# Planning the order of all engines through the attention of a two-layer hybrid transformer, with two modulation blocks moved into the merge

## The chip, the cores and the metric

The kernel runs on one core of one Trainium2 chip. The metric is device time in microseconds (us): the median over runs of one launch, from the first instruction to the last. Five engines work side by side: TensorE (PE in the profile: matrix products, with PEld for its weight loads), VectorE (DVE), ScalarE (ACT), GpSimd (POOL) and SyncE (SP), which here only issues DMAs. Each engine takes its instructions in the order in which the program lists them, and waits on semaphores for the others.

## The reference

Two layers over 512 latent tokens and 256 context tokens of width 1024, in float32. Cut to what matters:

```python
for l in range(DEPTH):                                   # DEPTH = 2
    mod = silu_c @ w_mod[l] + b_mod[l]                   # 1024 -> 6*1024, and mod_c from silu_cc for the context
    sh1, sc1, g1, sh2, sc2, g2 = jnp.split(mod[:, None, :], 6, axis=-1)
    h = modulate(rms_norm(x, norm1[l]), sh1, sc1)        # and hc from ctx
    na_q, na_k, na_v, gq, gk, gv, ga, gb = jnp.split(h @ w_in[l], IN_SPLITS, axis=-1)
    ya = neighbourhood attention of 8 heads              # windows of 8x16 on the 64-wide grid, bias, all context keys
    qb = apply_rope(rms_norm(heads(gq), q_gain[l]))      # kb likewise, from gk
    yb = grouped-query attention of 8 heads on 2 key heads
    x = x + g1 * ((sigmoid(ga) * (ya @ w_pa[l]) + sigmoid(gb) * (yb @ w_pb[l])) @ w_o[l])
    # the same for the context tokens, in layer 0 only
    h2 = modulate(rms_norm(x, norm2[l]), sh2, sc2)
    x = x + g2 * swiglu(h2, w_ffn_in[l], w_ffn_out[l])   # and the context, in layer 0 only
return rms_norm(x, final_norm)
```

`mod` is a matrix product with one row: each of its 48 blocks of 128 outputs is a weight block of 512 KB.

## The kernel before

**Products.** Each float32 operand is split into a high and a low part, and a product is three matmuls: high by high, high by low, low by high. For a weight, `weight` loads `wr`, ACT copies it to `wh` (L369), and POOL subtracts to give `wl` (L371; the first key weight of layer 1 goes through `kh` on ACT, L1277, and `kl` on DVE, L1278). `steps` (L384) issues the matmuls, in the order `h,wh`, `hl,wh`, `h,wl` for each of 8 blocks of 128 rows.

**Stages.** Per layer: normalization and first keys, attention, merge of the two branches with `w_pa` and `w_pb` (`pp`, `mb`, L1585), output projection, and the feed-forward part (FFN: `qu`, `qv`, `qc` in, `po` out). In layer 0 the columns are 512 latent and 256 context tokens, in layer 1 the queries are the latent ones only.

**Attention.** A stream of attention items gives scores (`sc`), on DVE the maximum per row (`m`, L1048, times the row factor `hr`, L1054), on ACT the exponential with its sum (`p`, L1056), on DVE the scaling by the reciprocal (`rc`, `p`), on PE the transposes (`tp`), on ACT and DVE their high and low halves (`pth` L1016, `ptl` L1017), and on PE the product with the values (`y`). Between these, the class `Flow` puts the matmuls of the projections that later heads need ("fillers": `pj`, `pv`, `k`, `v`, `q`, and the branch gates). Query and key vectors get a row factor from a sum of squares (`st` on PE, `hr` on DVE, a power on POOL, L807) and a rotation (`rope`: a shuffle `sh` on DVE, its product with `sin_sb`, on POOL or DVE, a product with `cos_sb` and an addition on DVE).

**What sets the order before.** `Flow` models the engines as lines of work and decides, as the program is written, which matmul comes next. Attention stands in a manual schedule for PE alone: PE's order is the written one, and the framework's scheduler places the instructions of the four other engines, as early as its own rules let them come.

**Modulation blocks.** A block of `wmodT` is reduced on DVE against the vector `crow`: two reductions of 128x1024 for each of layer 0's blocks in question (one for the latent, one for the context vector; L452), each followed by a read of the sum. `MODS` says after how many steps of the merge (first branch, second branch) and of the output projection how many blocks are reduced; layer 0 has 24 there, and the rest of the first 48 is reduced in the FFN, before its output needs the gate vector `G` (L478). The DMA of each block is issued by SP in the order of the rows.

Of the kernel before, what the change touches and what calls it, by code (L numbers as in the profile page):

```python
# [20 lines left out]
P = 128  # L21
D = 1024
KB = D // P
S = 512
# [46 lines left out]
MODS = (((0, 1, 1, 1, 1, 1, 0, 1), (1, 1, 2, 2, 2, 2, 1, 0), (1, 1, 1, 1, 1, 1, 1, 0)),  # L71
# [54 lines left out]


# [20 lines left out]
class Flow:  # L148
# [4 lines left out]
    def __init__(self, fillers, live, pace, hop, slow):  # L153
# [9 lines left out]
        self.lines = {e: Line() for e in "avg"}  # L163

# [3 lines left out]
    def go(self, t, *ops):  # L168

        for e, n in ops:  # L170
            fixed, each, on = RATE[e]
            t = self.lines[on].take(t + self.hop, (fixed + n * each) * self.slow["avg".index(on)])
        return t + self.hop
# [29 lines left out]
    def fill(self):  # L203
# [4 lines left out]
        if f.state == 0:  # L208
            next(f.steps)
# [4 lines left out]
        try:  # L214
            v = next(f.steps)
        except StopIteration:
# [8 lines left out]
        else:  # L225
            self.clock += v
# [5 lines left out]
    def ahead(self):  # L232

        for f in self.fillers:
            if f.state == 1:
                return
            if f.state == 0:
                next(f.steps)
                f.state = 1
                return  # L240

# [10 lines left out]
    def run(self, steps):  # L252
        mine = 0.0
        self.ahead()
        for v in steps:
            if isinstance(v, Until):
                self.wait(v.t)
            else:
                self.clock += v
# [8 lines left out]
    def force(self, ready):  # L268
        while not ready():
            if not self.fill():  # L270
                self.rest(self.clock + 0.5)

# [62 lines left out]
class Trunk:  # L335
    def __init__(self, tc, nc, dram):
        self.tc, self.nc, self.d = tc, nc, dram
# [12 lines left out]
    def ps(self, tag, n="ps", cols=512):  # L350
        if tag not in self.pbufs:
            tag = "a" if tag == "g" else "t" if "t" in self.pbufs else "n"
        return self.psum[tag].tile([P, cols], F32, tag=tag, bufs=self.pbufs[tag], name=self.name(n))
# [441 lines left out]
    def roped(self, t):  # L795
        return self.go(("v", S), ("g", S), ("v", S), ("v", S), at=t)
# [24 lines left out]
    def gqa_k(self, l, h, spans, pool, out):  # L821
# [25 lines left out]
        end = self.roped(flow.clock + 0.7)  # L847
        self.rope(kg, pool)
        yield Until(end - self.plan["soon"])
# [44 lines left out]
    def gqa_q(self, l, j, h, spans, pool, out):  # L894
# [14 lines left out]
        end = max(end, self.roped(flow.clock - 1.0))  # L909
        nr = self.small.tile([P, 16], F32, tag="hr", name=self.name("nr"))  # L910
        nc.vector.tensor_scalar(nr[:, : n // HD], r[:, : n // HD], -1.0, None, op0=ALU.mult)
        self.rope(qg, pool)
        yield Until(end - self.plan["soon"])
# [116 lines left out]
    def gqa_pair(self, head, q, kk, val, out, i, pool, done=None):  # L1030
# [20 lines left out]
        def exp(s, b, at):  # L1051
# [4 lines left out]
            nc.scalar.activation(p, s[:, :T], AF.Exp, bias=m[:, 0:1], scale=nr[:, c : c + 1], accum_out=m[:, 1:2])  # L1056
            self.soften(p, m[:, 1:2], pool)
            ps_.append(p)
            end = self.go(("v", 1), ("e", T), at=at)
# [27 lines left out]
    def ctx_item(self, head, score, val, out, r, nr, v, pool, done):  # L1087
# [4 lines left out]
        def soft(s, at):  # L1092
# [7 lines left out]
            for b in range(2):  # L1100
# [4 lines left out]
                self.soften(p[:, c], m[:, 2 + b : 3 + b], pool)  # L1105
            ps_.append(p)
            end = self.go(("v", S), ("v", 1), ("e", 256), ("e", 256), at=at)
            return end, self.go(("v", 1), ("v", 1), ("w", 256), ("w", 256), at=end - 0.5)
# [45 lines left out]
    def na_pair(self, head, q, k, val, bias, out, i, pool, done=None):  # L1154
# [16 lines left out]
        def soft(s, b, at):  # L1171
# [7 lines left out]
                halves(z[:]), halves(s[:, 0:512]), add, 1.0, BIG, ALU.add, ALU.min, m[:, 0:1])  # L1179
# [1178 lines left out]
```

## Time and profile before

| | |
|---|---|
| time, median of 3 runs | 1950.61 us (1950.57 to 1950.74) |
| the profiled execution | 1951.55 us; its span 1949.8 us, so 1.75 us lie around it |
| PE busy | 1913.6 us, 98% of the span |
| DVE, ACT, POOL busy | 1472.3, 943.6, 226.7 us |
| mean granted clock of PE | 0.995 |

Layer 0's attention lies at about 67 to 427 us of the span, its merge at 427 to 544, its FFN at 612 to 1135; layer 1's attention lies at about 1135 to 1458. A row of the timeline has the start and the duration in us, the engine, the line, the operation and its tiles (`out<-in`), and in brackets how long the engine had been idle and which instruction ended that. A row of the windows has the window, its length, then for each engine the busy time and the number of instructions, and behind them the clock that PE was granted (1.00 is full speed), the share of the DMA engines and the rate. A matmul's duration in the rows includes its filling of the array, so that the next starts before it ends: the step from start to start is what it costs.

### The profile page before, as it was taken

Reading aid. Unit: us, or ns where it says so; the run is one execution under the profiler, and the core shown is the slowest. Engines: PE = TensorE matmul, PEld = TensorE weight load, DVE = VectorE, ACT = ScalarE, POOL = GpSimd, SP = SyncE. Lnnn points to the kernel's source line nnn. Section 1 sums busy time; section 2 is a strip of 40 time slices with the busy share of each in tenths; the row PEclk is TensorE's granted clock in tenths of the full one; section 3 lists DMA queues with packets and bytes.
Section 4 is the critical chain, followed back from the end, with each engine's and each line's share of the span. In section 5 each row is a group of like instructions: output and inputs, shape, how many; then the busy total and the mean of one; then the engine's idle time right before and its main releaser. Section 6 shows DMA issues by size and latency. Waiting matters only on the chain.

```text
span 1949.8 us, 31489 instructions
## 1 busy us (share of the span) xinstructions
PE 1913.6 (98%) x12298; PEld 1778.2 (91%) x12298; DVE 1472.3 (76%) x2802; ACT 943.6 (48%) x1822; POOL 226.7 (12%) x131
## 2 busy tenths in 40 slices
PE   8999999999999989999999998999999999999998
PEld 8989999998899989999999888889988999999998
DVE  7468887769778877787868577888657688777785
ACT  5466666642236523342424345666553355444553
POOL 0332222214200000000000012322310000000000
PEclk9999999999999999999999999999999999999999
DMA  8121112234452143334443411121235532332332
GB/s 327 44 70 43 51 59 63 76 114 162 161 212 87 66 130 109 117 122 133 138 141 134 158 65 55 47 60 55 79 103 172 201 109 74 100 115 92 102 98 83
DMA packets 71669, 210.85 MB, mean 108 GB/s; under 512 B 8544, under 2 KB 10720, under 8 KB 71520
## 3 DMA queue, kind: packets, MB, share of 16 engines
q1 hardware_dynamic: 71520, 208.84, 32.6%
q8 instruction: 96, 1.57, 0.3%
q14 instruction: 53, 0.43, 0.1%
HBM read 196.75 MB, written 6.82 MB: 104 GB/s over the span
## 4 chain that ended last, share of the span: by engine, by line
PE 91%; DVE 5%; issue 2%; ACT 1%; DMA 1%; SPq 0%; POOL 0%; DVEq 0%; POOLq 0%; ACTq 0%
PE po L384 21%; PE pj L384 19%; PE qu L1740 14%; PE qv L1740 7%; PE pp L384 6%; PE qc L1740 3%; PE pv L957 3%; PE pf L384 3%; PE y L1076 2%; PE sc L1040 2%; PE tp L1066 2%; PE y L1203 2%; PE sc L1167 2%; PE tp L1191 1%; PE pj L680 1%
## 5 line engine op out<-in xcount | busy, mean ns | idle before, releaser
L1740 PE MATMUL qu<-r,w 128*128 128x384 f32 (+1 forms) x1872 | 295.0, 310 | 0.0
L1740 PEld LDWEIGHTS qu<-r,w 128*128 128x128 f32 x1872 | 281.1, 190 | 3.6 <-DVE tt L2219 2.4
L384 PE MATMUL pj<-h,wh 128*128 128x512 f32 (+1 forms) x704 | 257.4, 366 | 3.3 <-ACT kg L816 1.7
L384 PE MATMUL pj<-h,wl 128*128 128x512 f32 (+1 forms) x704 | 247.6, 352 | 0.0
L384 PE MATMUL pj<-hl,wh 128*128 128x512 f32 (+1 forms) x704 | 247.1, 351 | 0.0
L384 PE MATMUL po<-ph,wh 128*128 128x512 f32 (+1 forms) x576 | 198.4, 344 | 5.9 <-ACT wh L1907 5.9
L369 ACT ACTIVATE wh<-wr 128x1024 fp32r<-128x1024 f32 (+1 forms) x131 | 124.6, 954 | 161.2 <-issue 44.6
L384 PE MATMUL po<-ph,wl 128*128 128x512 f32 (+1 forms) x576 | 197.3, 343 | 0.0
L384 PE MATMUL po<-pl,wh 128*128 128x512 f32 (+1 forms) x576 | 197.0, 342 | 0.0
L1603 ACT ACTIVATE w<-wr 128x512 fp32r<-128x512 f32 x234 | 145.5, 625 | 103.9 <-DVE wr L2183 37.2
L371 POOL TENSOR_TENSOR wl<-wr,wh 128x1024 fp32r<-128x1024 f32 (+1 forms) x67 | 151.1, 2261 | 370.7 <-ACT wh L369 370.6
L1595 DVE SCALAR_TENSOR_TENSOR x<-po,G,x 128x256 f32<-128x256 f32 (+3 forms) x168 | 99.4, 597 | 102.5 <-PE po L384 101.3
L1607 DVE TENSOR_TENSOR w<-wr,w 128x512 fp32r<-128x512 f32 x234 | 159.3, 686 | 10.7 <-ACT w L1603 9.8
L1740 PE MATMUL qv<-r,w 128*128 128x384 f32 (+1 forms) x936 | 150.7, 310 | 0.3 <-ACT tt L1746 0.3
L384 PEld LDWEIGHTS pj<-h,wl 128*128 128x128 f32 x704 | 133.4, 189 | 18.0
L384 PEld LDWEIGHTS pj<-h,wh 128*128 128x128 f32 x704 | 133.7, 190 | 17.5 <-ACT kg L816 1.9
L384 PEld LDWEIGHTS pj<-hl,wh 128*128 128x128 f32 x704 | 133.9, 190 | 13.5
L1740 PEld LDWEIGHTS qv<-r,w 128*128 128x128 f32 x936 | 141.2, 190 | 0.5 <-ACT tt L1746 0.5
L1016 ACT ACTIVATE pth<-tp 128x512 fp32r<-128x512 f32 x176 | 103.2, 595 | 65.7 <-PE tp L1066 37.5
L512 POOL TENSOR_TENSOR rs<-rs,expo 128x2 f32<-128x2 f32 (+2 forms) x8 | 6.2, 773 | 1106.8 <-DVE rs L511 1106.8
L1017 DVE TENSOR_TENSOR ptl<-tp,pth 128x512 fp32r<-128x512 f32 x176 | 119.4, 684 | 18.4 <-ACT pth L1016 16.9
L384 PEld LDWEIGHTS po<-ph,wh 128*128 128x128 f32 x576 | 109.0, 189 | 18.9 <-ACT wh L1907 6.1
(255 smaller groups left out, 4331.5 us busy)
## 6 DMA issues: line engine op xcount, KB each, us to landing
wr<-wfi SPq DMA_DIRECT2D x88, 512.0 KB, 3.3
wr<-wmodT SPq DMA_DIRECT2D x84, 512.0 KB, 3.4
wr<-win SPq DMA_DIRECT2D x68, 512.0 KB, 3.4
wr<-wfo SPq DMA_DIRECT2D x64, 256.0 KB, 2.7
wr<-wo SPq DMA_DIRECT2D x26, 512.0 KB, 4.2
wr<-wp SPq DMA_DIRECT2D x32, 256.0 KB, 2.8
x<-x SPq DMA_DIRECT2D x16, 384.0 KB, 7.1
wr<-wmod SPq DMA_DIRECT2D x12, 512.0 KB, 7.2
```

The lines of the kernel that those rows point to most:

```text
L369: nc.scalar.activation(hi, raw, AF.Copy)
L371: (eng or nc.gpsimd).tensor_tensor(lo, raw, hi[:].bitcast(F32), op=ALU.subtract)
L384: nc.tensor.matmul(ps[:, : b - a], u[:, c], v[k][:, a:b], start=(k == 0 and i == 0), stop=(k == nk - 1 and i == 2),)
L957: nc.tensor.matmul(ps[:, t * 256 : t * 256 + 256], a[k][:, tok], b[:, c], start=(k == 0 and i == 0), stop=(k == KB - 1 and i == 2))
L1016: nc.scalar.activation(hi, tp, AF.Copy)
L1017: nc.vector.tensor_tensor(lo, tp, hi[:].bitcast(F32), op=ALU.subtract)
L1040: nc.tensor.matmul(s[:, lo:up], qt[:, b * P : (b + 1) * P], kk[k][:, lo:up], start=(k == 0 and (b % 2 == 0 or lo > 0)), stop=(k == 1), ski ...
L1066: nc.tensor.transpose(tp[:, (2 * j + b) * P : (2 * j + b + 1) * P], ps_[b][:, (k + j) * P : (k + j + 1) * P], self.ident)
L1595: self.nc.vector.scalar_tensor_tensor(x[j][:, f:u], ps[:, f - a : u - a], self.G[l][i][:, s, j : j + 1], x[j][:, f:u], op0=ALU.mult, op1=A ...
L1603: self.nc.scalar.activation(t[:, :n], src, AF.Copy)
L1607: self.nc.vector.tensor_tensor(t[:, n : 2 * n], src, t[:, :n].bitcast(F32), op=ALU.subtract)
L1740: nc.tensor.matmul(banks[bank], u[:, c], v, start=(first and k == 0 and i == 0), stop=(k == kn - 1 and i == 2), skip_group_check=True)
```

## The change

The change has two parts.

One: two of layer 0's modulation blocks, which are reduced in the FFN before, go into the merge (one in its first branch, one in its second), so 26 instead of 24 stand ahead of the FFN.

Two: the attention of each layer is first recorded. While `attend` runs, every instruction goes to a `Plan` instead of the program. `Plan.add` gives it a cost by a formula, and a time by its inputs, and what `Flow` asks of the lines now comes from these records. Then `Plan.emit` gives each instruction a due time, worked backwards from when PE needs it. PE and SP keep their recorded order. DVE, ACT and POOL are listed by simulation: of what could start first (within 0.15 us), the earliest due. All five engines start at time 0 of that simulation. The rows are then written in that order, in a manual schedule for all five engines. The attention's instructions of the changed kernel therefore all carry the line L481.

```diff
-MODS = (((0, 1, 1, 1, 1, 1, 0, 1), (1, 1, 2, 2, 2, 2, 1, 0), (1, 1, 1, 1, 1, 1, 1, 0)),
+MODS = (((0, 1, 1, 1, 1, 1, 1, 1), (1, 2, 2, 2, 2, 2, 1, 0), (1, 1, 1, 1, 1, 1, 1, 0)),
...
-            with tc.manual_schedule(engines={mybir.EngineType.PE}):
-                flow.run(self.attend(items))
+            nc.plan = flow.plan
+            flow.run(self.attend(items))
+            nc.plan = None
+            every = {getattr(mybir.EngineType, e) for e in ("PE", "DVE", "Activation", "Pool", "SP")}
+            with tc.manual_schedule(engines=every):
+                flow.plan.emit()
...
+    def emit(self):
+        ops, n = self.ops, len(self.ops)
...
+        due = [0.0] * n
+        for i in reversed(range(n)):
+            o = ops[i]
+            due[i] = o["at"] if o["lane"] == "p" else min(
+                [due[j] - o["cost"] - 0.1 for j in then[i]], default=o["at"] + 20.0)
...
+        queue = {e: [i for i, o in enumerate(ops) if o["lane"] == e] for e in "ps"}
+        can = {e: {i for i, o in enumerate(ops) if o["lane"] == e and not left[i]} for e in "avg"}
+        clock = dict.fromkeys("pavgs", 0.0)
...
+        for _ in range(n):
+            best = None
+            for e in "pavgs":
+                some = queue[e][:1] if e in queue else can[e]
+                times = [(max(t, clock[e]), i) for i in some for t in (begins(i),) if t is not None]
+                if times:
+                    first = min(times)[0]
+                    d, t, i = min((due[i], t, i) for t, i in times if t <= first + 0.15)
+                    if best is None or (t, i) < best[:2]:
+                        best = t, i, e
...
+        for i in sorted(range(n), key=lambda i: (start[i], i)):
+            ops[i]["run"](*ops[i]["args"], **ops[i]["kw"])
```

**At the end of layer 0's FFN input, on DVE.** `wr` are the loaded modulation blocks, each of which `mod` needs twice, and `G` is the gate vector that `po`'s use waits for. Before:

```order
L452 ISA wr1410_7770,mod0_105<-wr1410_7770,crow1010_5169 128x1024
...
L452 ISA junk1011_5170,mod0_105<-wr1413_7792,crow1010_5169 128x1024
...
L452 ISA wr1413_7792,mod0_105<-wr1413_7792,crow1010_5169 128x1024
...
L452 ISA junk1011_5170,mod0_105<-wr1414_7796,crow1010_5169 128x1024
...
L452 ISA wr1414_7796,mod0_105<-wr1414_7796,crow1010_5169 128x1024
...
L452 ISA junk1011_5170,mod0_105<-wr1415_7800,crow1010_5169 128x1024
...
L452 ISA wr1415_7800,mod0_105<-wr1415_7800,crow1010_5169 128x1024
...
L465 TENSOR_TENSOR mod0_105<-mod0_105,bmod_sb_86 128x8 x2
L478 TENSOR_SCALAR G0_1_112<-mod0_105 128x8 x2
L2223 TENSOR_TENSOR ph1400_7707<-ph1400_7707,qu1391_7651 128x384
```

And now:

```order
L664 ISA junk1011_5170,mod0_105<-wr1412_7778,crow1010_5169 128x1024
...
L664 ISA wr1412_7778,mod0_105<-wr1412_7778,crow1010_5169 128x1024
...
L664 ISA junk1011_5170,mod0_105<-wr1415_7800,crow1010_5169 128x1024
...
L664 ISA wr1415_7800,mod0_105<-wr1415_7800,crow1010_5169 128x1024
...
L677 TENSOR_TENSOR mod0_105<-mod0_105,bmod_sb_86 128x8 x2
L690 TENSOR_SCALAR G0_1_112<-mod0_105 128x8 x2
L2440 TENSOR_TENSOR ph1402_7715<-ph1402_7715,qu1393_7659 128x384
```

Of the four last blocks two are left; the two others are reduced in the merge.

**At the start of layer 0's attention, on POOL.** `wl86` is the low half of the first weight of the attention's projections (`pj99` on PE), `sh` a part of the rotation, `hr88` a power. Before:

```order
L791 TENSOR_TENSOR sh109_780<-sh109_780,sin_sb_93 128x512
L371 TENSOR_TENSOR wl86_660<-wr84_656,wh85_658 128x1024
L371 TENSOR_TENSOR wl95_694<-wr93_690,wh94_692 128x1024
L371 TENSOR_TENSOR wl98_700<-wr96_696,wh97_698 128x1024
L807 TENSOR_TENSOR hr88_669<-hr88_669,expo_100 128x12
L371 TENSOR_TENSOR wl105_766<-wr103_762,wh104_764 128x1024
```

And now:

```order
L481 TENSOR_TENSOR hr88_658<-hr88_658,expo_100 128x12
L481 TENSOR_TENSOR sh106_676<-sh106_676,sin_sb_93 128x512
L481 TENSOR_TENSOR wl86_656<-wr84_654,wh85_655 128x1024
L481 TENSOR_TENSOR wl95_665<-wr93_663,wh94_664 128x1024
L481 TENSOR_TENSOR wl98_668<-wr96_666,wh97_667 128x1024
L481 TENSOR_TENSOR hr104_674<-hr104_674,expo_100 128x12
```

The power and the rotation's product now stand ahead of the weight's low half.

**At the same place on ACT.** `wh85` is the high half of that weight, and the `v` rows take the transposed values (`tv`) from PE. Before:

```order
L369 ACTIVATE wh85_658<-wr84_656 128x1024
L815 ACTIVATE sq77_531<-pj79_542 128x256
L816 ACTIVATE kg76_530<-pj79_542,gain_sb_90 128x256
L369 ACTIVATE wh94_692<-wr93_690 128x1024
L867 ACTIVATE vt78_537<-pj82_571 128x256
L369 ACTIVATE wh97_698<-wr96_696 128x1024
L815 ACTIVATE sq81_547<-pj83_598 128x256
L816 ACTIVATE qg80_546<-pj83_598,qgain_102 128x256
L891 ACTIVATE v89_672<-tv91_674 128x4x64
```

And now:

```order
L1027 ACTIVATE sq81_547<-pj83_598 128x256
L1028 ACTIVATE qg80_546<-pj83_598,qgain_102 128x256
L481 ACTIVATE v89_659<-tv91_661 128x4x64
L481 ACTIVATE v89_659<-tv92_662 128x2x64
L481 ACTIVATE v90_660<-tv91_661 128x4x64
L481 ACTIVATE v90_660<-tv92_662 128x2x64
L481 ACTIVATE wh85_655<-wr84_654 128x1024
L481 ACTIVATE wh94_664<-wr93_663 128x1024
```

The high half was ahead of the squares of a last piece and now stands behind the four value rows.

**At the start of layer 1's attention, on DVE.** `kl2009` and `kl2010` are the low halves of the first key weight (`pj2027` on PE), and `st2017` and `st2011` are sums from PE. Before:

```order
L538 SCALAR_TENSOR_TENSOR hl1972_11489<-x1175_6210,mod1_106,h1971_11488 128x512
L1278 TENSOR_TENSOR kl2009_11805<-wr2006_11801,kh2007_11803 128x512
L491 TENSOR_TENSOR acc1974_11513<-acc1974_11513,sq1976_11535 128x256
L1278 TENSOR_TENSOR kl2010_11806<-wr2006_11801,kh2008_11804 128x512
L1278 TENSOR_TENSOR kl2023_11843<-wr2020_11839,kh2021_11841 128x512
L1278 TENSOR_TENSOR kl2024_11844<-wr2020_11839,kh2022_11842 128x512
L491 TENSOR_TENSOR acc1974_11513<-acc1974_11513,sq1978_11558 128x256
```

And now:

```order
L481 TENSOR_SCALAR hr2012_11805<-st2011_11804 128x8
L481 TENSOR_SCALAR rs2028_11821<-st2017_11810 128x2
L481 TENSOR_TENSOR sh2016_11809<-sh2016_11809,sin_sb_93 128x512
L481 TENSOR_TENSOR qg2001_11743<-qg2001_11743,cos_sb_92 128x512
L481 TENSOR_TENSOR qg2001_11743<-qg2001_11743,sh2016_11809 128x512
L481 COPY rx2030_11823<-hr2012_11805 128x512
L481 TENSOR_SCALAR hr2014_11807<-st2013_11806 128x8
L481 TENSOR_TENSOR q2033_11826<-qg2001_11743,q2033_11826 64x512
L481 TENSOR_TENSOR kl2009_11802<-wr2006_11799,kh2007_11800 128x512
L481 TENSOR_TENSOR kl2010_11803<-wr2006_11799,kh2008_11801 128x512
```

The low halves stood among the sums of squares of layer 0's last rows, and now stand behind the first rotation.

**Late in layer 1's attention, on DVE.** `ptl` is the low half of the transposed weights, for which PE's products with the values wait, and `k2328`, `k2329` (now `k2346`, `k2347`) are keys of the neighbourhood attention. Before:

```order
L936 TENSOR_TENSOR k2328_13321<-pj2293_13168,k2328_13321 64x512
L1048 TENSOR_REDUCE m2314_13271<-sc2313_13262 128x1
L1048 TENSOR_REDUCE m2315_13273<-sc2313_13262 128x1
L936 TENSOR_TENSOR k2329_13324<-pj2293_13168,k2329_13324 64x512
L1054 TENSOR_TENSOR m2314_13271<-m2314_13271,hr2091_12267 128x1
L1017 TENSOR_TENSOR ptl2322_13293<-tp2320_13287,pth2321_13292 128x512
L1054 TENSOR_TENSOR m2315_13273<-m2315_13273,hr2091_12267 128x1
L1027 TENSOR_TENSOR y2306_13221<-y2323_13296,ys2324_13309 64x256
L1017 TENSOR_TENSOR ptl2327_13318<-tp2325_13312,pth2326_13317 128x512
L1009 RECIPROCAL rc2317_13278<-m2314_13271 128x1
L1010 TENSOR_SCALAR p2316_13276<-p2316_13276,rc2317_13278 128x768
```

And now, at the first columns of the same kind of keys:

```order
L481 TENSOR_TENSOR k2346_12139<-pj2330_12123,k2346_12139 64x512
L481 TENSOR_TENSOR ptl2351_12144<-tp2349_12142,pth2350_12143 128x512
L481 TENSOR_REDUCE m2353_12146<-sc2352_12145 128x1
L481 TENSOR_REDUCE m2354_12147<-sc2352_12145 128x1
L481 TENSOR_TENSOR m2353_12146<-m2353_12146,hr2293_12086 128x1
L481 TENSOR_TENSOR m2354_12147<-m2354_12147,hr2293_12086 128x1
L481 TENSOR_TENSOR k2347_12140<-pj2330_12123,k2347_12140 64x512
L481 RECIPROCAL rc2356_12149<-m2353_12146 128x1
L481 TENSOR_SCALAR p2355_12148<-p2355_12148,rc2356_12149 128x768
L481 RECIPROCAL rc2358_12151<-m2354_12147 128x1
L481 TENSOR_SCALAR p2357_12150<-p2357_12150,rc2358_12151 128x768
L481 TENSOR_TENSOR ptl2365_12158<-tp2363_12156,pth2364_12157 128x512
```

Before, a `ptl` stands behind two reductions, two key rows and a product with `hr`; now a `ptl` stands ahead of the reductions, the next one behind the whole softmax of a block.

209 lines of the change are left out of this document (187 added, 22 removed).

## The prediction

> **What bounds the kernel now.** I read the page first, then the clock and busy time of chosen windows, then the timeline at each place where the tensor engine (PE) stops.
>
> ```profile
> PE 1913.6 (98%) x12298; PEld 1778.2 (91%) x12298; DVE 1472.3 (76%) x2802; ACT 943.6 (48%) x1822; POOL 226.7 (12%) x131
> PE 91%; DVE 5%; issue 2%; ACT 1%; DMA 1%; SPq 0%; POOL 0%; DVEq 0%; POOLq 0%; ACTq 0%
> ```
>
> PE is busy in 98% of the span and holds 91% of the chain that ends last. The change takes no matmul away, so all it can win is time in which PE is idle or its clock is down. The windows show where that is (length, then PE's busy time first; the clock stands behind POOL).
>
> ```profile
> core 0: us, PE busy (x) PEld busy (x) DVE busy (x) ACT busy (x) POOL busy (x), PEclk, DMA share, GB/s
> 67.00:427.00 360.00, 356.43 (x2492) 329.64 (x2492) 271.77 (x610) 220.63 (x477) 91.94 (x50) 1.00 0.21 65
> 450.00:475.00 25.00, 25.00 (x142) 21.89 (x141) 24.95 (x39) 2.96 (x4) 9.31 (x5) 1.00 0.50 184
> 718.00:725.00 7.00, 3.44 (x8) 2.72 (x9) 6.20 (x14) 2.40 (x4) 0.00 (x0) 0.51 0.34 101
> 1175.00:1225.00 50.00, 44.98 (x316) 41.39 (x315) 36.19 (x76) 29.73 (x60) 15.98 (x8) 0.97 0.22 69
> 1225.00:1315.00 90.00, 85.35 (x524) 74.51 (x525) 72.49 (x147) 56.45 (x109) 24.50 (x14) 0.98 0.16 47
> 1287.00:1291.50 4.50, 2.59 (x23) 2.39 (x22) 4.38 (x9) 3.44 (x7) 0.00 (x0) 1.00 0.03 9
> 1291.50:1295.50 4.00, 4.00 (x20) 3.72 (x19) 2.39 (x6) 1.27 (x3) 0.00 (x0) 0.57 0.00 0
> ```
>
> Idle PE time is 360 - 356.43 = 3.6 us in layer 0's attention, 5.0 in 1175 to 1225 and 4.65 in 1225 to 1315 (layer 1's attention). Twice here a stop is followed by a stretch at about half clock. In 718 to 725, PE's 8 matmuls take 3.44 us, 0.43 each, where the rows of the third part step by 0.23: 8 x 0.20 = 1.6 us lost besides the stop. I use 1.6 for each stretch of this kind.
>
> **The change, part by part.**
>
> *The gate in layer 0's FFN.* DVE reduces its last four blocks, and only then come `G` and what PE waits for:
>
> ```profile
> 710.82 1.23 DVE L452 CUSTOM_DVE_ANT_0 junk<-wr,crow 128x1024 f32<-128x1024 f32 x1 [1.57 <-DMA wr<-wmodT]
> 713.23 0.08 DVE L452 DVE_READ_ACCUMULATOR2_ANT mod<- 128x1 f32 x1
> 716.67 1.22 DVE L452 CUSTOM_DVE_ANT_0 junk<-wr,crow 128x1024 f32<-128x1024 f32 x1 [0.94 <-DMA wr<-wmodT]
> 719.41 0.25 DVE L478 TENSOR_SCALAR G<-mod 128x8 f32<-128x8 f32 x2
> 715.37 0.28 PE L384 MATMUL po<-ph,wl 128*128 128x256 f32 x1
> 721.56 0.80 PE L384 MATMUL po<-ph,wh 128*128 128x512 f32 x1 [5.91 <-ACT wh L1907]
> ```
>
> The order rows leave `wr1412` and `wr1415` where `wr1410`, `wr1413`, `wr1414`, `wr1415` stood, and on SP their loads take the places of the first two. So the last reduction ends where the second block's did, at 713.3, and `G` comes near 713.5. From `G` to PE it took 721.56 - 719.41 = 2.15 us, so PE could go on at 715.65, which is when it runs dry (715.37 + 0.28). The 5.9 us go, and the half-clock stretch with them: -7.5. If the second block's load is as late as it was here, this is already in the 713.3; each us that it comes later costs one.
>
> *The merge.* The two blocks are 4 reductions of 1.22 us, 4.9 us, on a DVE that is full (24.95 of 25 us in 450 to 475). Their two loads of 512 KB take the SP places behind other blocks' loads, at a DMA share of 0.50. Ahead of the first `mb` DVE has room, and later PE has little:
>
> ```profile
> 420.83 2.89 DVE L397 TENSOR_TENSOR lo<-yb,hi 128x768 fp32r<-128x768 f32 x3 [1.95 <-ACT hi L396]
> 426.70 1.23 DVE L444 SCALAR_TENSOR_TENSOR junk<-junk,crow 128x1024 f32<-128x1024 f32 x1 [1.12 <-ACT junk L443]
> 430.32 0.69 DVE L1585 SCALAR_TENSOR_TENSOR mb<-gt,pp 128x512 f32<-128x512 f32 x1 [1.66 <-PE pp L384]
> 467.68 0.67 DVE L1585 SCALAR_TENSOR_TENSOR mb<-gt,pp 128x512 f32<-128x512 f32 x1
> 469.17 0.40 PE L384 MATMUL pj<-h,wh 128*128 128x512 f32 x1
> ```
>
> The new order lists `crow` ahead of the `lo` rows and five reductions ahead of the first `mb` (one before), so the idle 1.95 + 1.12 + 1.66 = 4.7 us can be filled. Up to the last wide `mb`, 19 reductions stand where 16 did, 3 x 1.22 = 3.7 us more. PE needs that bank for the `pj` at 469.17, 0.8 us after `mb` ends. The ends: 0, when the idle time is filled, and 3.7 - 0.8 = 2.9. It is nearer to 0, since 4.7 exceeds 3.7; I take +0.5. In the FFN, four reductions fewer win nothing beyond the gate, since PE waits for DVE nowhere else there for long.
>
> *The start of layer 0's attention.* In the plan all engines start at time 0, while in truth PE is still busy with the stage before and the others have time. So weights that were split in that time now stand in strict order behind work that waits for PE:
>
> ```profile
> L371 POOL TENSOR_TENSOR wl<-wr,wh 128x1024 fp32r<-128x1024 f32 (+1 forms) x25 | 57.7, 2310 | 159.3 <-ACT wh L369 159.2
> L807 POOL TENSOR_TENSOR hr<-hr,expo 128x12 f32<-128x12 f32 x5 | 12.1, 2421 | 15.4 <-DVE hr L806 15.4
> L791 POOL TENSOR_TENSOR sh<-sh,sin_sb 128x512 f32<-128x512 f32 x4 | 5.7, 1419 | 24.8 <-DVE sh L790 14.0 <-DVE m L1054 10.8
> 66.65 0.17 DVE L806 TENSOR_SCALAR hr<-st 128x12 f32<-128x12 f32 x1 [5.29 <-PE st L804]
> 68.02 0.55 ACT L891 ACTIVATE v<-tv 128x256 fp32r<-128x256 f32 x2 [0.22 <-DVE v L892]
> 67.55 0.40 PE L384 MATMUL pj<-hl,wh 128*128 128x512 f32 x1
> 67.79 0.40 PE L384 MATMUL pj<-h,wl 128*128 128x512 f32 x1
> 68.02 0.40 PE L384 MATMUL pj<-h,wh 128*128 128x512 f32 x1
> ```
>
> POOL now begins with the power of `hr88`, which exists from 66.82 on: 66.82 + 2.42 + 1.42 (`sh`) + 2.31 (`wl86`) = 72.97. PE wanted `wl86` at 67.79 and had it. That is a stop of 5.2 us. On ACT `wh85` now follows the four `v` rows, which end at 68.57; it then has 2.1 us until POOL turns to `wl86` at 70.66, so it costs nothing more. The next weights need 2.31 us each and PE uses one for over 5.5 us (24 steps of 0.23), so POOL is ahead again after one. With a half-clock stretch behind it: +5.2 + 1.6 = +6.8.
>
> *The start of layer 1's attention.* The same with the key weight:
>
> ```profile
> 1133.25 0.62 ACT L1277 ACTIVATE kh<-wr 128x512 fp32r<-128x512 f32 x1
> 1139.37 0.69 DVE L1278 TENSOR_TENSOR kl<-wr,kh 128x512 fp32r<-128x512 f32 x1
> 1150.08 0.69 DVE L793 TENSOR_TENSOR qg<-qg,sh 128x512 f32<-128x512 f32 x1
> 1152.10 1.27 ACT L918 ACTIVATE q<-qg 64x512 fp32r<-64x512 f32 x2
> 1154.38 0.43 DVE L1331 COPY rx<-hr 128x512 f32<-128x512 f32 x1
> 1152.89 0.58 PE L502 MATMUL st<-ones,acc 128*128 128x1 f32 x4
> 1153.88 0.39 PE L384 MATMUL pj<-h,kl 128*128 128x512 f32 x1
> ```
>
> `kl` was ready 14 us early. Now `rs2028` waits for the `st` that ends at 1153.47 and ends about 1153.6; then three rotation rows (0.69 each, 0.02 overlap, about 2.05), `rx` 0.43, a small row 0.17, `q2033` 0.69, whose ACT half and `kh` (0.64 + 0.62) fit beside, and `kl2009` 0.69: 1157.6. PE wanted `kl` at 1153.88: +3.7, and +1.6 for the clock: +5.3.
>
> *Inside the attention.* Here the plan places DVE by PE's need. One stop of before shows what it can win:
>
> ```profile
> 1289.31 0.69 DVE L936 TENSOR_TENSOR k<-pj,k 64x512 fp32r<-64x512 f32 x1
> 1290.23 0.69 DVE L1017 TENSOR_TENSOR ptl<-tp,pth 128x512 fp32r<-128x512 f32 x1
> 1290.97 0.66 PE L1066 MATMUL tp<-ident_sb,p 128*128 128x128 f32 x4 [1.91 <-DVE ptl L1017]
> ```
>
> `ptl` stood behind rows that nobody awaited, and PE stopped 1.9 us. The new order puts a `ptl` ahead of such rows, but the next one behind a whole softmax. In 1225 to 1315 there are 4.65 us idle and 1.6 of clock to win, at most 6.25; at the other end nothing, or a loss of the same size if the new rows stand worse. I take -5.0, near the upper end, since the stops there are of this one kind. In 1175 to 1225 the chain from score to exponential is itself longer than its cover, and order cannot shorten it: 0. Layer 0 has 3.6 us: I take two thirds, -2.4.
>
> The sum: -7.5 + 0.5 + 6.8 + 5.3 - 5.0 - 2.4 = -2.3. The profiled execution becomes 1951.55 - 2.3 = 1949.25; it lies 0.94 above the median, so the median becomes 1950.61 - 2.3 = 1948.3. That is within 0.2% (3.9 us), about what a measurement of this kernel can tell from no change.
>
> **The rivals.**
>
> *B: full clock after both new stops.* Before, a stop of 1.9 us (window 1287 to 1291.5) was followed by clock 0.57; but the two new stops may lie so that the clock stays up. Then 3.2 us less: 1945.1. For it: each stop's place against the clock's windows is unknown. Against it: both are longer than 1.9 us. The Trainium skill (TensorE: Matmul & The Clock Gate, What's actually happening) has the clock halve after at least one idle window of about 3.4 us. By that rule both stops' clock could stay up (the one of layer 0 is cut in two by the first two matmuls), and the sum would be 1945.1 instead of 1948.3; the 1.9 us row, with 0.57 behind it, speaks against the rule here.
>
> *C: the new stops are paid back.* A PE held up by 5.2 and 3.7 us gives the engines that nobody delays a lead, and PE's waits after it shrink: the 5.0 us and 1.6 of clock in 1175 to 1225 go, and the last 1.2 of layer 0. -7.8 more: 1940.5. Against it: those waits hang on PE's own scores and projections, which are late with it.
>
> *D: slower, by DVE's rows of a softmax in one piece.* Two maxima, two products, two reciprocals and two scalings now stand together, and the reciprocals wait for ACT's exponentials; a `ptl` behind them waits too.
>
> ```profile
> L1017 DVE TENSOR_TENSOR ptl<-tp,pth 128x512 fp32r<-128x512 f32 x176 | 119.4, 684 | 18.4 <-ACT pth L1016 16.9
> ```
>
> At 0.04 us of PE per `ptl` that is 176 x 0.04 = 7 us, which turns -2.3 into +4.7; from there it decides. I price it at 0.05: +8.8, 1957.1. For it: DVE is 72.49 of 90 us busy in 1225 to 1315, with little room to catch up. Against it: PE has fillers between the rows.
>
> *E: the gate stays*, since the last block's load is as late as before (it ended 0.94 us of DVE's waiting): +7.5, 1955.8.
>
> **How the numbers follow.** The forecast as summed has 0.43 (its own range 1944 to 1953), B 0.15, C 0.17, D 0.18, E 0.07. Faster by over 0.2% (below 1946.7): C 0.17, 0.12 of B, 0.13 of the forecast, together 0.42. Slower (above 1954.5): 0.15 of D, 0.05 of E, 0.04 of the forecast, together 0.24. Within: 0.34. The range 1938 to 1957 reaches from below C to D's price and leaves out about 0.1 on each side.
>
> **What would show it.** Right: no PE stop near 715 and clock 1.00 there; a stop of about 5 us near 67 us behind POOL's `wl`, one of 3 to 4 us at the first `kl` of layer 1, half clock behind each; fewer and shorter waits for `ptl`. Wrong: PE going on at 67 as before; a wait for `pp` or `mb` near 470; many new short waits of `y` for `ptl`.

## The result, and the profile after

The changed kernel takes 2078.64 us (median of 4 runs, 2074.66 to 2080.79) against 1950.59 us of the kernel before in the same comparison: the ratio is 1.0646, 95% interval [1.0633, 1.066]. The forecast was 1948.3 us, in a range of 1938 to 1957. The page of the changed kernel, in the lines that answer to those of before:

```profile
PE 1953.9 (94%) x12298; PEld 1799.0 (87%) x12298; DVE 1494.1 (72%) x2802; ACT 946.7 (46%) x1822; POOL 224.9 (11%) x131
PE 60%; DVE 7%; DMA 2%; ACT 1%; issue 1%; SPq 0%; POOL 0%; DVEq 0%; ACTq 0%; POOLq 0%
```

The span grew by 126.5 us (1949.8 to 2076.3), while PE's busy time grew by 40 and its share fell from 98% to 94%. The windows tell in which stages. First the changed kernel: layer 0's attention, layer 1's attention, layer 0's output projection, layer 0's FFN.

```profile
core 0: us, PE busy (x) PEld busy (x) DVE busy (x) ACT busy (x) POOL busy (x), PEclk, DMA share, GB/s
67.00:502.00 435.00, 380.85 (x2491) 342.96 (x2491) 287.37 (x615) 223.88 (x480) 99.20 (x53) 0.96 0.17 55
1206.00:1585.00 379.00, 329.77 (x2024) 290.37 (x2023) 250.55 (x534) 190.47 (x385) 78.83 (x45) 0.96 0.17 55
619.00:690.00 71.00, 69.07 (x402) 68.38 (x402) 52.55 (x92) 30.45 (x47) 0.85 (x1) 1.00 0.50 175
690.00:1205.00 515.00, 514.19 (x2951) 488.15 (x2950) 401.66 (x695) 207.05 (x372) 1.86 (x2) 1.00 0.38 121
```

The last three of these stages in the kernel before (layer 0's attention took 360 us there):

```profile
1135.00:1458.00 323.00, 312.89 (x2021) 280.77 (x2020) 240.13 (x534) 187.67 (x385) 79.43 (x45) 0.99 0.21 64
544.00:612.00 68.00, 68.00 (x399) 67.97 (x399) 52.28 (x91) 30.23 (x46) 0.85 (x1) 1.00 0.50 178
612.00:1135.00 523.00, 516.59 (x2960) 490.92 (x2959) 407.31 (x706) 208.19 (x374) 1.86 (x2) 0.99 0.37 121
```

The FFN became 8 us shorter and the output projection 3 longer; the two attentions became 75 and 56 us longer. PE has the same matmuls in them (x2491 against x2492). It is idle for 435 - 380.85 = 54 us in layer 0's attention and 49 in layer 1's, where it was idle for 3.6 and 10, and the clock is at 0.96. What PE waited for (total, times, longest):

```profile
PE sc L481 <- DVE m L481: 66.0, 58, 4.0
PE pj L481 <- DVE ql L481: 9.1, 4, 3.9
PE tp L481 <- DVE ptl L481: 5.9, 5, 2.2
...
PE pj L481 <- ACT kh L481: 3.4, 1, 3.4
PE tp L481 <- DVE z L481: 3.0, 2, 2.0
PE pj L481 <- POOL wl L481: 2.9, 2, 2.7
...
PE pj L481 <- ACT wh L481: 2.2, 1, 2.2
```

One wait stands out: the scores for `m`, 58 times. Before, this wait is not in the list at all. The timeline shows one, PE and then DVE:

```profile
160.30 1.09 PE L481 MATMUL sc<-kk,q 128*128 128x512 f32 x6
162.45 0.73 PE L481 MATMUL sc<-kk,q 128*128 128x512 f32 x2 [1.05 <-DVE m L481]
161.43 0.96 DVE L481 TENSOR_REDUCE m<-sc 128x1 f32<-128x768 f32 x1 [1.88 <-PE sc L481]
163.21 0.96 DVE L481 TENSOR_REDUCE m<-sc 128x1 f32<-128x768 f32 x1 [0.82 <-PE sc L481]
```

A score tile has two blocks of 768 columns, written by eight matmuls. Six are done, then DVE reduces the first block (columns 0 to 767 of the tile) to `m`, and only when that has ended do the last two matmuls (columns 1024 to 1535) start. Before, the same eight ran through:

```profile
168.12 1.56 PE L1040 MATMUL sc<-kk,q 128*128 128x512 f32 x8
```

The two orders of PE's rows show it too. These are rows five to eight of one tile, first before, then now, with the wait of the row in brackets; the buffer numbers differ:

```
L1040 MATMUL sc127_966<-kk122_926,q119_863 128x256
L1040 MATMUL sc127_966<-kk123_927,q119_863 128x256
L1040 MATMUL sc127_966<-kk122_926,q119_863 128x512
L1040 MATMUL sc127_966<-kk123_927,q119_863 128x512

L481 MATMUL sc126_696<-kk121_691,q111_681 128x256
L481 MATMUL sc126_696<-kk122_692,q111_681 128x256
L481 MATMUL sc126_696<-kk121_691,q111_681 128x512 [waits DVE_49]
L481 MATMUL sc126_696<-kk122_692,q111_681 128x512
```

The plan writes all rows sorted by their planned start, and by its own bookkeeping of columns the reduction may start after the fourth matmul. So its row comes between the sixth and the seventh, and the seventh, which comes later in the program and writes into the same tile, gets a wait on it.

### The profile page after: what moved, and what is told of

It reads as the page before. It is cut to its first block, busy times and chain, and to the rows that moved or that the text cites. A ratio compares the mean times of both kernels' runs of the same rounds, so it can differ in the third digit from the quotient of the medians.

```text
span 2076.3 us, 31443 instructions
## 1 busy us (share of the span) xinstructions
PE 1953.9 (94%) x12298; PEld 1799.0 (87%) x12298; DVE 1494.1 (72%) x2802; ACT 946.7 (46%) x1822; POOL 224.9 (11%) x131
## 4 chain that ended last, share of the span: by engine, by line
PE 60%; DVE 7%; DMA 2%; ACT 1%; issue 1%; SPq 0%; POOL 0%; DVEq 0%; ACTq 0%; POOLq 0%
PE po L596 20%; PE qu L1957 13%; PE qv L1957 7%; PE pj L481 4%; PE qc L1957 3%; PE pj L596 3%; PE pf L596 3%; PE pp L596 2%; PE sc L481 2%; PE pv L481 1%; PE y L481 1%; PE tp L481 1%; DVE m L481 1%; DVE z L481 1%; DMA wr<-win 1%
## 5 line engine op out<-in xcount | busy, mean ns | idle before, releaser
L481 PE MATMUL pj<-h,wh 128*128 128x512 f32 (+1 forms) x512 | 193.8, 378 | 14.3 <-DVE ql L481 9.1
L481 PE MATMUL pj<-h,wl 128*128 128x512 f32 (+1 forms) x512 | 183.1, 358 | 2.9 <-POOL wl L481 2.9
L481 PE MATMUL pj<-hl,wh 128*128 128x512 f32 (+1 forms) x512 | 182.6, 357 | 0.0
L481 ACT ACTIVATE pth<-tp 128x512 fp32r<-128x512 f32 x176 | 103.7, 596 | 126.2 <-PE tp L481 125.0
L481 DVE TENSOR_TENSOR ptl<-tp,pth 128x512 fp32r<-128x512 f32 x176 | 119.5, 687 | 51.6 <-ACT pth L481 50.3
L481 POOL TENSOR_TENSOR wl<-wr,wh 128x1024 fp32r<-128x1024 f32 x44 | 107.6, 2455 | 276.1 <-ACT wh L481 255.9
L581 ACT ACTIVATE wh<-wr 128x1024 fp32r<-128x1024 f32 (+1 forms) x85 | 75.9, 898 | 129.6 <-issue 31.4
L481 PEld LDWEIGHTS pj<-h,wh 128*128 128x128 f32 x512 | 100.3, 196 | 23.8 <-issue 7.9
L596 PEld LDWEIGHTS po<-ph,wl 128*128 128x128 f32 x576 | 108.3, 188 | 14.0
L596 PEld LDWEIGHTS po<-pl,wh 128*128 128x128 f32 x576 | 108.6, 189 | 12.8
```

The source lines that it names most:

```text
L481: ops[i]["run"](*ops[i]["args"], **ops[i]["kw"])
L581: nc.scalar.activation(hi, raw, AF.Copy)
L596: nc.tensor.matmul(ps[:, : b - a], u[:, c], v[k][:, a:b], start=(k == 0 and i == 0), stop=(k == nk - 1 and i == 2),)
```

## The experiments

The theory at this point (T): the place of the reduction's row in the program, not its place in any engine's queue, makes PE wait. The first rivals: the new orders of the other engines are too slow in themselves (R), or the two blocks in the merge are (M). In the comparisons below the kernel before took 1951.6 to 1953.0 us.

### The same queues, another place in the program

```diff
+        score = [t for t in self.users if t.startswith("sc")]
+        for t in score:
+            wrote = [i for i in self.users[t] if ops[i]["lane"] == "p"]
+            for i in self.users[t]:
+                if ops[i]["lane"] != "p":
+                    before[i].update(w for w in wrote if w < i)
...
-        for i in sorted(range(n), key=lambda i: (start[i], i)):
+        for i in sorted(range(n), key=lambda i: (at[i], i)):
```

`before` also holds the inputs, each engine's order and the reuse of buffers, and `at` is the planned start, raised until it lies behind all of `before`.

> The changed kernel with one difference: every engine keeps the same instructions in the same order, but in the written program the reduction of a score tile's first block stands behind all eight matmuls of that tile, not between the sixth and the seventh. Theory T (PE waits at the seventh matmul because the first block's reduction is written ahead of it and reads the same tile, although other columns): the 66 us of waits of sc for m go, and most of the 55 us of extra half-clock time with them (some 25 us of loss), so 1965 to 1995 us. Rival R (the new orders of DVE, ACT and POOL are themselves too slow, and the wait of sc only shows the lateness): the orders are the same, so 2060 to 2080 us, with the waits at other places. Rival M (the two modulation blocks in the merge cost it): 2078 us.

Measured: 2022.96 us, ratio 1.0363 [1.0349, 1.0376], so 56 us below the changed kernel. The wait is gone, and others have grown:

```profile
PE tp L507 <- DVE ptl L507: 16.1, 11, 6.3
PE pj L507 <- DVE ql L507: 11.0, 4, 4.8
...
PE sc L507 <- DVE m L507: 1.9, 1, 1.9
```

T holds for the wait: 66.0 us became 1.9. But its time was 28 us too low, and half of the loss is still there. So is nearly all of the half-clock time that T counted as a consequence: 67 us, against 75 in the changed kernel and 20 before (summed over the span from the traces' clock records). R is right for that half.

### The wait alone, in the kernel before

```diff
                 for n, score in enumerate(cur.scores):
                     score[0](s[:, n * w : n * w + w])
                     ends.append(flow.clock + (n + 1) * cur.cost[0])
+                    if n == 0:
+                        ends[0] = score[1](s[:, 0:w], ends[0])
```

(and the same step is left out of the loop behind it)

> The kernel before, PE's order unchanged, with only this: the reduction (or the addition of the bias with its minimum) of a score tile's first block is written ahead of the second block's matmuls; nothing is planned. Theory T: PE waits once per score tile, 1.0 to 1.3 us each, some 64 to 72 times, and part of the stops pull the clock down: 2015 to 2060 us, with waits of sc for m of 60 to 90 us. Rival R: no wait follows from where a row is written, 1946 to 1956 us.

Measured: 2076.28 us, ratio 1.0628 [1.0613, 1.0643]. With no plan at all, the written place of this one kind of row costs as much as the whole change, and more than the 2015 to 2060 us that T expected. What PE waited for, and one of the waits:

```profile
PE sc L1040 <- DVE m L1048: 40.5, 32, 2.9
PE sc L1167 <- DVE m L1178: 35.6, 32, 4.3
PE sc L1138 <- DVE p L1010: 14.3, 4, 4.3
PE sc L1148 <- ACT p L1103: 7.5, 4, 1.9
161.35 0.86 PE L1040 MATMUL sc<-kk,q 128*128 128x512 f32 x4
163.26 0.97 PE L1040 MATMUL sc<-kk,q 128*128 128x256 f32 x4 [1.05 <-DVE m L1048]
```

Here the second block waits as a whole, 72 times, 97.9 us. The waits for `m` alone, 76.1 us, lie in the expected range; the tiles of the context (14.3 + 7.5) wait for a longer chain. The 124 us also hold the clock's answer: it stood at half for 75 us of the span, against 20 before. By the prediction's 1.6 us for 3.44 at half clock that is an estimated 26 us, and 97.9 + 26 = 124.

### The blocks and the plan apart

```diff
-MODS = (((0, 1, 1, 1, 1, 1, 0, 1), (1, 1, 2, 2, 2, 2, 1, 0), (1, 1, 1, 1, 1, 1, 1, 0)),
+MODS = (((0, 1, 1, 1, 1, 1, 1, 1), (1, 2, 2, 2, 2, 2, 1, 0), (1, 1, 1, 1, 1, 1, 1, 0)),
```

> The kernel before with only the two modulation blocks moved into the merge; nothing is planned. Theory T: the stop at the gate goes (5.9 us and 1.6 of half clock) and the merge costs at most 0.5, so 1943 us (1942 to 1946). Rival M: slower by tens of us. Rival that the gate stays bound by the load of the last block: 1950 us.

Measured: 1950.19 us, ratio 0.9982 [0.997, 0.9995], above the 1942 to 1946 expected. The runs fall into two groups: five of twelve lie at 1943.8 to 1945.2, in the range, and seven at 1949.5 to 1954.6. The profiled run is of the second group. The stop at the gate is gone from its list of waits. In its place stands one at layer 0's output projection, which was not there before (PE, then DVE ahead of it):

```profile
552.08 0.52 PE L384 MATMUL po<-mh,wl 128*128 128x384 f32 x1 [2.45 <-DVE wl L371]
549.66 1.22 DVE L452 CUSTOM_DVE_ANT_0 junk<-wr,crow 128x1024 f32<-128x1024 f32 x1 [3.40 <-DMA wr<-wmodT]
550.81 1.22 DVE L371 TENSOR_TENSOR wl<-wr,wh 128x1024 fp32r<-128x1024 f32 x1
```

DVE, which makes this weight's low half here (not POOL), is not busy: it stands idle for 3.40 us until the next modulation block is loaded, and `wl` comes behind that block's reduction in its order. SP had issued the load at 546.29, right behind the reduction before it. In the kernel before, DVE waits 3.38 us for such a load at the same place, but its `wl` starts at 545.39, 5.4 us earlier. So `wl` hangs on a chain of loads and reductions here, and comes late when the chain does. The opposite, the plan with the old table:

> The changed kernel with the old table of modulation blocks (two blocks back in the FFN), the attention planned as in the change. Theory T and rival R: the gate's stop is back, 2084 to 2088 us. Rival M: 1950 us.

Measured: 2082.5 us, ratio 1.0663 [1.0649, 1.0678], 4 us above the changed kernel and a little under the expected 2084. M falls by both.

### PE's order without the planned order of the others

```diff
-            every = {getattr(mybir.EngineType, e) for e in ("PE", "DVE", "Activation", "Pool", "SP")}
-            with tc.manual_schedule(engines=every):
-                flow.plan.emit()
+            with tc.manual_schedule(engines={mybir.EngineType.PE}):
+                for op in flow.plan.ops:
+                    op["run"](*op["args"], **op["kw"])
```

> The changed kernel without the planned order: what was recorded is written in the order of recording, in a manual schedule for PE alone, as before the change; PE's order is word for word that of the changed kernel, and the two blocks are in the merge. Theory U (behind the score wait, the rest of the loss, 2023 against 1952 us, comes from the planned order of the four other engines): 1938 to 1955 us. Rival P (the new timing in Flow gives PE a worse order): 1985 us or more.

Measured: 1969.95 us, ratio 1.0095 [1.0077, 1.0114]. It lies between the two expectations: 53 us below the first experiment (U), but 20 above the kernel with the blocks alone. From that it differs in the timing by which `Flow` chooses PE's order (P) and, for the context's tiles, in the written place of the softmax scalings. Layer 0's attention takes 13 us longer than before and layer 1's 7; PE is idle for 12 us in the first, where 3.6 were idle before.

```profile
67.00:440.00 373.00, 361.08 (x2501) 331.61 (x2501) 271.54 (x615) 221.20 (x480) 92.70 (x50) 1.00 0.20 63
```

### Which of the fixed orders

From the first experiment's kernel, the list of engines in the manual schedule was cut.

```diff
-            every = {getattr(mybir.EngineType, e) for e in ("PE", "DVE", "Activation", "Pool", "SP")}
+            every = {getattr(mybir.EngineType, e) for e in ("PE", "Activation", "Pool", "SP")}
```

> As e1_listed (score tiles written whole ahead of their readers), but DVE is left out of the manual schedule, so the framework places DVE's rows; PE, ACT, POOL and SP keep the planned order. Theory V (DVE's planned rows are what is left: a softmax in one piece ahead of the ptl and ql that PE waits for): most of the 70 us goes, 1955 to 1975 us. Rival Q (the planned orders of ACT, POOL and SP, with the late weight halves at the starts): 2005 to 2025 us.

Measured: 2007.49 us, ratio 1.0286 [1.0271, 1.0302]. With `("PE", "DVE")` in that place:

> As e1_listed, but only PE and DVE keep the planned order; the framework places ACT, POOL and SP. Theory V: still 2000 to 2025 us, with the long waits for ptl and ql. Rival Q: 1950 to 1970 us, and no stop at 67 us.

Measured: 2010.18 us, ratio 1.0297 [1.0282, 1.0313]. V and Q both fail as the whole cause: each part, set free alone, wins 13 to 15 us, and each theory met its range once: 2007.49 lies in Q's, 2010.18 in V's. With `("PE",)`, so that only the place of the rows in the program is planned:

> As e1_listed, written in the planned order, but only PE is in the manual schedule; DVE, ACT, POOL and SP are placed by the framework. Theory V2 (the fixed orders of the four engines together cost the 53 us between e5_recorded and e1_listed; each holds the others up): 1965 to 1980 us, like e5_recorded. Rival L (the framework follows the order in which rows are written, so that the planned listing spoils its placing too): 1990 to 2015 us.

Measured: 1970.63 us, ratio 1.009 [1.0076, 1.0104], the same as with the recorded order. So the place of the rows does no harm once the score tiles are written whole, and the fixed orders of the four engines cost 2022.96 - 1970.63 = 52 us together. The parts do not add up: DVE's order fixed alone beside PE's costs 2010.18 - 1970.63 = 40 us, and the orders of ACT, POOL and SP without DVE's 2007.49 - 1970.63 = 37. Either half is enough for most of the loss. Some 21 of the 52 us are the clock by the same estimate: it stood at half for 67 us with all orders fixed and for 22 with PE's alone. The first experiment's timeline has one of the waits that make this up (ACT, POOL, DVE, then PE):

```profile
178.38 0.85 ACT L507 ACTIVATE q<-qg 64x768 fp32r<-64x768 f32 x1 [2.75 <-DVE qg L507]
180.19 0.99 ACT L507 ACTIVATE p<-sc,m,nr 128x768 f32<-128x768 f32 x1
182.14 0.59 ACT L507 ACTIVATE pth<-tp 128x512 fp32r<-128x512 f32 x1
180.25 3.15 POOL L507 TENSOR_TENSOR wl<-wr,wh 128x1024 fp32r<-128x1024 f32 x1 [2.51 <-ACT wh L507]
181.50 2.32 DVE L507 TENSOR_SCALAR p<-p,rc 128x768 f32<-128x768 f32 x1
184.47 0.69 DVE L507 TENSOR_TENSOR ptl<-tp,pth 128x512 fp32r<-128x512 f32 x1
185.21 1.11 PE L507 MATMUL tp<-ident_sb,p 128*128 128x128 f32 x4 [6.28 <-DVE ptl L507]
```

ACT waits 2.75 us for a rotated query (`qg`), whose `q` PE uses first at 206.8; behind it in the fixed order stand the exponentials and then `pth`. On DVE a scaling stands ahead of `ptl`; it took 2.32 us beside a `wl` on POOL, and the next one, after POOL had ended, 0.62. PE stops for 6.3 us, though its next transposes take scaled exponentials (`p`) that had been ready since 175.5 us; they waited only until `pth` and `ptl` had read an earlier tile.

### Better plans

A plan that takes the score tile as one region in its own bookkeeping:

```diff
+        if ap.name.startswith("sc"):
+            return 0, P, 0, 1536
```

> The changed kernel with a plan that takes a score tile as one region, so that in its simulation too the reduction comes after all eight matmuls; all five engines in the planned order. Theory T: the waits of sc for m go as in e1_listed. Theory V: since the plan's costs and its rule of the earliest due are otherwise the same, it ends like e1_listed, 2005 to 2035 us. Rival W (the plan went wrong only because it did not know that wait): 1940 to 1965 us.

Measured: 2008.32 us, ratio 1.0293 [1.0278, 1.0309]. W falls: knowing the wait is not enough. (`Flow` reads the same bookkeeping, so PE's order changes here as well, and this is not the first experiment's order.) Then, on top of it, PE starting later in the simulation:

```diff
-        clock = dict.fromkeys("pavgs", 0.0)
+        clock = dict(p=8.0, a=0.0, v=0.0, g=0.0, s=0.0)
```

> As e8_plan_whole, but in the plan's simulation PE starts at 8 us and the other engines at 0, so that the first weight halves (wl86, kl2009) come ahead of rows that wait for PE. Theory S (the two stops at the starts are the price of starting all engines at 0: in the changed kernel 2.4 + 3.1 us at 67 us and 3.4 us at the first kh, with half clock behind each): 2008 minus 9 of stops and 3 to 6 of clock, 1992 to 1998 us. Rival: the lateness moves to the rows now listed behind (the power for hr88), within 4 us of 2008.

Measured: 2002.46 us, ratio 1.0257 [1.0243, 1.0272]. The wait for `kh` is gone, and 0.7 us for the first `wh` and 1.7 for its `wl` stay: ACT still takes a rotated query (`q`) ahead of `wh`, and POOL, which now has `wl` ahead of the power, can begin it only at 69.64, when `wh` is done. So 6 to 7 us are won where 10 to 16 were expected: S names the right mechanism, but too large a price. Three more edits looked for the rest: letting an engine wait for an earlier-due row (`t <= first + 0.8` for `0.15`, on the plan of e8), then, on the plan of e9, costs 1.25 times as large for DVE, ACT and POOL, and SP left to the framework.

> As e8_plan_whole, but the plan may let an engine wait for an earlier-due row that can start within 0.8 us of the first possible one, instead of 0.15 us. Theory V3 (a row that is not urgent gets ahead because it can start 0.2 us earlier, and holds up ptl or ql): faster than e8_plan_whole by 10 to 30 us. Rival (the order is right by the plan's times, but the chip's times drift from them, through longer rows on DVE and POOL): within 8 us of it.

> As e9_plan_start, but in the plan's simulation every row of DVE, ACT and POOL costs 1.25 times as much, so that the planned order leaves room for lateness. Theory D1 (the fixed orders cost time since the chip's rows are slower or later than the plan has them): 1975 to 1992 us against 2002 of e9_plan_start. Rival D2 (no even margin helps, since a fixed order is late wherever one row of it is late): within 8 us of 2002.

> As e9_plan_start, with the rows of DVE, ACT and POOL unchanged, but SP's DMAs are placed by the framework. Theory D3 (the recorded order of the DMAs makes loads late, such as the bias for which POOL waits 53.5 us in the changed kernel, and POOL's rows behind it hold up DVE and ACT): 1970 to 1990 us. Theory D2: within 6 us of 2002.

Measured: 2067.17 us, ratio 1.0589 [1.0573, 1.0605]; 2031.31 us, 1.0391 [1.0367, 1.0414]; 1997.03 us, 1.0229 [1.0215, 1.0243]. The first two made it worse, by 59 and 29 us. So V3 and D1 fall, and so do their rivals, which expected no change; why these two plans lose more is not shown (with the wider window PE waits 27 times for `ptl` at its transposes, 35.1 us, against 10 times and 13.4 us on e8's plan). The DMAs' order is 5 us and not the cause, so D3 falls too.

### The blocks, one by one

From the kernel before, one block in the merge instead of two:

```diff
+MODS = (((0, 1, 1, 1, 1, 1, 1, 1), (1, 1, 2, 2, 2, 2, 1, 0), (1, 1, 1, 1, 1, 1, 1, 0)),
```

> The kernel before with one modulation block moved into the merge (first branch) instead of two. By the gate: one block of 2.4 us and perhaps its DMA wait less in the FFN, so the stop falls from 5.9 to 2.5 to 3.5 us; by the merge: two reductions instead of four, so the 2.4 us that PE waits for a low weight half at the output projection in e2_mods_only falls to 0 to 1. 1944 to 1950 us on a chip where before takes 1950.6. If the gate is bound by the last block's load: no gain against before.

Measured: 1949.63 us, ratio 0.999 [0.9981, 0.9999]. Its gate still stops PE for 1.7 us; in the output projection its profiled run, the slowest of its runs, waits 3.8 us in two stops for `wl`, which was expected at 0 to 1. There too DVE stands idle for a block's load ahead of the `wl`, for 4.18 us. With a second block behind the last step of the output projection:

```diff
+MODS = (((0, 1, 1, 1, 1, 1, 1, 1), (1, 1, 2, 2, 2, 2, 1, 0), (1, 1, 1, 1, 1, 1, 1, 1)),
```

> The kernel before with two blocks moved out of the FFN, one into the merge's first branch and one behind the last step of the output projection, instead of two into the merge. By e2_mods_only the merge's price is a wait of 2.4 us for a low weight half at the output projection, with half clock in some runs; by e11_mods_one one block there costs less. 1942 to 1947 us where before takes 1951 to 1952; if the block behind the output projection delays the norm after it, 1950 us or more.

Measured: 1947.85 us, ratio 0.9975 [0.9966, 0.9984], the only version here whose gain over the kernel before exceeds 0.2%, and faster than the changed kernel by 6%. From 420 to 720 us PE waits for three things only:

```profile
PE po L384 <- ACT mh L1589: 0.6, 1, 0.6
PE pj L384 <- DVE t L1587: 0.5, 1, 0.5
PE po L384 <- DVE wl L371: 0.2, 1, 0.2
```

The two tables are the same up to the last step of the output projection, and yet the `wl` that came late with one block, starting at 551.12 us, starts at 547.12 here. So the chain's time differs between runs of the same rows, and part of the 2.45 and 3.8 us above is the run and not the table. The median is 0.25% under the kernel before, where the 1942 to 1947 expected were 0.2 to 0.5% under it. Its interval overlaps that of the two blocks in the merge, so which of the two tables is better is not shown.

## Why the prediction was wrong

**The sum by the runs.** From the changed kernel to the kernel before, in four steps: the place of the reduction's row 2078.6 - 2023.0 = 56 us; the fixed orders of the four engines 2023.0 - 1970.6 = 52; PE's order by the new timing 1970.6 - 1950.2 = 20; the two blocks -2. Together 126. The steps come from three comparisons, with the kernel before moving by 2 us between them.

**The gate: right.** No wait is left at the gate, and the FFN took 515 us instead of 523: 8, where -7.5 stood in the sum.

**The merge: mis-sized, by the wrong wait.** The term was +0.5, taken near 0. It was worked out from DVE's busy time at the `pj` near 469 us. With the blocks alone PE waited 0.9 us there, at 470.5, and for POOL's `wl`, not for `mb`. The larger stop came 83 us after 469, as 2.45 us for a weight's low half that stood on DVE behind a block whose load was late. The sum named the two added loads and put no time to them. How much of the stop is theirs and how much the run's is not separated. The output projection of the changed kernel took 3 us more. With that the blocks alone win 2 us and not 7 by the median, though five of the twelve runs lie 7 to 8.5 us under the median of the kernel before.

**The two starts: right in place and nearly in size.** The rows of the changed kernel:

```profile
69.30 0.79 PE L481 MATMUL pj<-h,wh 128*128 128x512 f32 x1 [2.24 <-ACT wh L481]
73.19 0.80 PE L481 MATMUL pj<-h,wl 128*128 128x512 f32 x1 [2.67 <-POOL wl L481]
1227.69 0.79 PE L481 MATMUL pj<-h,kh 128*128 128x512 f32 x1 [3.36 <-ACT kh L481]
69.00:79.00 10.00, 7.03 (x16) 5.06 (x17) 8.71 (x4) 3.82 (x5) 9.97 (x5) 0.51 0.34 107
1226.00:1233.00 7.00, 5.31 (x12) 3.97 (x13) 6.18 (x11) 4.40 (x7) 1.64 (x1) 0.52 0.00 0
```

2.24 + 2.67 = 4.9 us where 5.2 stood, though in two pieces: that `wh85` would cost nothing, since POOL was busy anyway, held only for the sum. 3.4 us where 3.7 stood, but for another row: PE waited for `kh`, which ACT takes behind the first rotated query and which the sum let fit beside, not for DVE's `kl`. That the size fits is partly luck. Half clock came with both (0.51 from 69 to 79 us, 0.52 from 1226 to 1233), so rival B fell. Both stretches were longer than the 1.6 us in the sum had it: an estimated 2.6 to 3 us each, by PE's steps of 0.43 instead of 0.23. With them the two starts cost about 14 us where 12.1 stood.

**Inside the attention: the step that failed.** The terms -5.0 and -2.4 became losses of some 114 us (56 + 52 + 20, less about 14 us of the starts, which the fixed orders hold). Three things were missed. First, the sum priced only the rows that change their place on an engine. The eight matmuls of a score tile still stand in the same order, and the sum put nothing to a wait that they might gain; the order of PE's rows with its waits shows that wait. Second, DVE's rows were judged by one example in which `ptl` came to stand well. Rival D named the softmax in one piece, and in the traces `ptl` and `ql` are what PE waits for; but D had it at 8.8 us, at 0.05 us for each `ptl`, a price that no run shows, and its sign, many short waits of `y` for `ptl`, did not come (twice, 1.3 us, in the changed kernel). The waits are few and long, of `tp` and `pj`. By the runs DVE's fixed order alone costs 40 us; but setting it free alone gives back only 15 of the 52, since the orders of the other three cost 37 without it. Third, PE's own order was taken as unchanged in effect. It is 20 us worse.

Rival C, that a held-up PE meets fewer waits, fell: the waits after the starts grew. E fell with the gate.

**What stays open.** Why the fixed orders lose 52 us is shown only as far as that either half, DVE's or that of the three others, is enough for most of it: neither wider costs, nor waiting for urgent rows, nor the DMAs' order explains it. The chain at 178 to 185 us is one instance, and its share is not measured. What in `Flow`'s new timing makes PE's order 20 us worse was not taken apart. That the framework tracks a score tile as one whole follows from the wait and the columns of the code; tiles cut in two were not tried.

## What to carry to other kernels

When rows are written in a new order, compare the waits of every engine's rows, not only their places: a reader that is written between two writers of one tile makes the second writer wait, even for other columns, and 1 us at 58 places outweighed all that had been planned. An order fixed for all engines at once lets one late row hold up urgent ones on every engine; fix the order of the engine that bounds the kernel, and try the others one at a time. Work moved off a gate into another stage brings its loads along, and they can hold up rows far behind the place where it is put; so follow that engine's order, with the loads that it waits for, to the next row that PE needs.

## What the runs showed of the hardware that was not expected

Single stops of 1.05 us, evenly spread, mostly left the clock up, while longer ones among them pulled it down: in the changed kernel it stood at half for 75 us of the span, in stretches of 3.4 us and multiples of it, against 20 before (the trace's clock records). In the 3.4 us ahead of each of its 15 stretches PE had been idle for 1.8 us or more; windows of that length with a single stop of 1.05 us were not followed by half clock. With the wait alone in the kernel before, two stretches began behind 0.76 and 1.05 us, so 1.8 is no firm limit. Those 55 us more at half speed explain an estimated 26 us of the loss, by the 8 x 0.20 us in 3.44 us that the prediction counted at the gate.
